# The last scan group inside the chunk loop, and the output projection behind it in another order

## The chip, the cores and the metric

The kernel runs on one core of a Trainium2 chip. Five engines matter: TensorE (PE, with its weight loads PEld), VectorE (DVE), ScalarE (ACT), GpSimd (POOL) and SyncE (SP), which issues most transfers. The metric is the device time of one execution in microseconds, taken as the median of several runs. Everything is float32; a product is made of three matmuls on split operands (high part and rest), which the tables call `fp32r`.

## The reference, cut to what matters

The model has two layers on 1024 tokens of width 1024. Layer 0 is a gated MLP; layer 1 is a Mamba-2 SSD mixer with 8 groups (G) of 4 heads and chunks of 128 tokens. The change is all in layer 1 and behind it:

```python
proj = h @ w_in                      # z (2048), x, B, C (4096), dt
xbc = silu(causal_conv(xbc))
# for each chunk: y = diagonal part + C @ state + x * d_skip, then state = state * decay + B' @ x
gated = (y * silu(z)).reshape(..., 8, 256)
gated = rmsnorm(gated, norm_w)       # over each group's 256 columns
h = h + gated @ w_out                # (1024 x 2048) @ (2048 x 1024)
return rmsnorm(h, final_norm_w)
```

The scan over the chunks is serial for each group. The output projection needs all groups, each scaled by its own norm.

## The kernel before, in words

**Projections and scan.** Groups 0, 1, 3, 5 have their projections made and stored earlier. For the groups in `plain` (2, 4, 6, 7) a generator, `projections()`, makes the x and B/C columns while the scan runs. It yields after every 6 matmuls of 128x512; the document calls that a *fill unit*. There are `total = 128` units, of which `AHEAD = 16` run before the loop. `scans()` loops over 7 groups x 8 chunks = 56 chunks. In each, `pe_b(n)` does the chunk's products (tiles `yy` and `sp`), one unit follows, then `pe_a(n+2)` transposes for a later chunk (`tp`), the state is updated (L1612), the output is formed (`out`), the decays of chunk n+1 are turned into weights (L1573, tile `wl`), and a second unit runs. `want` fixes this pace: (n + f) / 56 of the units left. The order on each engine is the order in which the code is written (`manual_schedule`).

**The last group.** Group 7 is not in the loop. Behind it `z_last` makes group 7's gate columns (tile `az`, 96 matmuls), `last_steps` scans its 8 chunks, and `interleave` mixes those with products 1 and 7 of the output projection.

**Output projection.** `Out` forms the 1024 x 2048 x 1024 product as seven products of half-size blocks (Strassen's scheme in Winograd's form), here in the order 1, 7, 2, 6, 4, 5, 3. A is the gated activations in quadrants A00 to A11 (first index: token half; tile `ya`), B the weights (tile `wb`). A product has four quarters (c), each of 4 x 2 x 3 = 24 matmuls into `bo`; product 3 is done by `last_mm`. `prep(n, c)` loads what is missing, scales A by the group's norm (L1816, tile `rb`) and splits both operands (L109 to L112). One quarter is prepared ahead. Sums of blocks are made by accumulating transfers from POOL's queue (`add` at L745, `b12_plus` at L708); plain loads are on SP's queue. The scale of a group goes a long way: squares, a sum over channels by matmul (`pr`), a store to `ss_d`, a load to `sv`, a root, a store to `rs_d`, and a load of `rb` spread over all partitions.

Of the kernel before, what the change touches and what calls it, by code (L numbers as in the profile page):

```python
# [29 lines left out]
def kernel(  # L30
# [627 lines left out]
    class Out:  # L658
# [10 lines left out]
        ORDER = (1, 7, 2, 6, 4, 5, 3)  # L669

        def __init__(self, src, w, scale, res, accs, keep, ran):
            self.src, self.w, self.scale, self.res, self.accs, self.keep = src, w, scale, res, accs, keep
            self.ran, self.had, self.late = ran, set(), []
# [11 lines left out]
        def load_a(self, i, kh, c):  # L685
# [5 lines left out]
            if self.scale is None:  # L691
                nc.sync.dma_start(out=raw, in_=src)
            else:
                self.scale(raw, src, g, i)
# [21 lines left out]
        def prep(self, n, c):  # L716
# [7 lines left out]
            x, y = A(i, j, c), B(k, l, c)  # L724
            xh, xl = (sb.tile([P, 2, 512], F32R, name=m, tag="wr", bufs=4) for m in ("xh", "xl"))
# [4 lines left out]
            if n == 1:  # L730
                self.add(x, self.src[c][:, :, 512:1024] if self.scale is None else A(1, 0, c))
                if self.scale is None:
                    if c % 2:
                        self.b12_plus(1, c // 2)
                elif c == 2:
                    self.b12_plus(1, 0)
            elif n == 7:
                if c == 0 and self.scale is not None:
                    self.b12_plus(1, 1)
# [7 lines left out]
        def sums(self, n, c):  # L747
# [7 lines left out]
            elif n == 4:  # L755
                if self.scale is not None:
                    if c % 2 == 0:
                        self.b12_plus(0, c // 2)
                    self.add(A(1, 0, c), A(1, 1, c))
                else:  # L760
                    if c == 1:
                        self.b12_plus(0, 1)
                    nc.vector.tensor_tensor(out=A(1, 0, c), in0=A(1, 0, c), in1=A(1, 1, c), op=ALU.add)

        def fetch(self, n, c):

            need = {1: (("a", 0, 0), ("b", 0, 0), ("b", 0, 1)), 11: (("a", 0, 0), ("b", 0, 0)),
                    2: (("a", 0, 1), ("b", 1, 0)), 22: (("a", 1, 1),), 4: (("b12", 0, 1),),
                    5: (("b", 1, 1),)}.get(n, ())
            if n in ((4,) if self.scale is None else (1, 11)):  # L770
                need += ("a", 1, 0),
            for kind, i, k in need:
                at = kind, i, k, c if kind == "a" else c // 2
                if at not in self.had:
                    self.had.add(at)
# [901 lines left out]
    def last_steps():  # L1677
# [8 lines left out]
        for c in range(8):  # L1686
            if c < 7:
                a(c + 1)
                yield
# [260 lines left out]
```

## Time and profile before

| | |
|---|---|
| median of 3 runs | 1596.49 us (1592.2 to 1597.92) |
| profiled execution | 1599.88 us |
| its span | 1598.2 us |
| TensorE / DVE / ACT / POOL busy | 1506.0 / 1055.3 / 777.0 / 418.7 us |
| chunk loop | from about 1069 to 1361 us |
| z projection of group 7 (`az`) | 1361 to 1392 us |
| output projection (`bo`) | 1392 to 1590 us |

Tables of stages give busy time and number of instructions for each engine. A group's row gives the line, engine, operation, output <- input, shape and count, then the total and mean duration, then the idle time ahead of it and what ended it. A busy TensorE is not one at its peak: matmuls overlap, so the spacing of their starts tells the pace.

### The profile page before, as it was taken

Reading aid. Unit: us, or ns where it says so; the run is one execution under the profiler, and the core shown is the slowest. Engines: PE = TensorE matmul, PEld = TensorE weight load, DVE = VectorE, ACT = ScalarE, POOL = GpSimd, SP = SyncE. Lnnn points to the kernel's source line nnn. Section 1 sums busy time; section 2 is a strip of 40 time slices with the busy share of each in tenths; the row PEclk is TensorE's granted clock in tenths of the full one; section 3 lists DMA queues with packets and bytes.
Section 4 is the critical chain, followed back from the end, with each engine's and each line's share of the span. In section 5 each row is a group of like instructions: output and inputs, shape, how many; then the busy total and the mean of one; then the engine's idle time right before and its main releaser. Section 6 shows DMA issues by size and latency. Waiting matters only on the chain.

```text
span 1598.2 us, 21253 instructions
## 1 busy us (share of the span) xinstructions
PE 1506.0 (94%) x7834; PEld 1239.8 (78%) x7834; DVE 1055.3 (66%) x1706; ACT 777.0 (49%) x1247; POOL 418.7 (26%) x443
## 2 busy tenths in 40 slices
PE   5799999999999999998999999989999999979988
PEld 4799988888888887876788787767777777757766
DVE  7966566666666554777637377757777767658656
ACT  4522233323222354555555455646766677544444
POOL 3601010000000131220011312126777765231231
PEclk7999999999999999999999999999999999989999
DMA  5153332332333999755367878776565665795992
GB/s 173 41 191 127 105 109 100 110 111 97 111 108 125 323 261 256 162 139 129 105 154 177 165 165 158 174 208 194 156 176 160 194 172 145 238 249 174 229 237 107
DMA packets 176919, 260.21 MB, mean 163 GB/s; under 512 B 16320, under 2 KB 102960, under 8 KB 173616
## 3 DMA queue, kind: packets, MB, share of 16 engines
q1 hardware_dynamic: 124992, 169.45, 34.3%
q0 software_dynamic: 41888, 71.58, 23.0%
q10 hardware_dynamic: 9936, 17.83, 3.1%
q8 instruction: 62, 1.02, 0.3%
q14 instruction: 41, 0.34, 0.1%
HBM read 185.61 MB, written 51.18 MB: 148 GB/s over the span
## 4 chain that ended last, share of the span: by engine, by line
PE 59%; issue 14%; DMA 9%; DVE 9%; ACT 6%; POOL 1%; ACTq 0%; SPq 0%; POOLq 0%; DVEq 0%
PE acc L136 10%; PE acc L134 9%; PE acc L135 9%; PE ab L134 4%; PE ab L136 4%; PE ab L135 4%; DMA ya<-ya 2%; PE yy L1582 2%; DMA wl<-cs_d 2%; PE yy L1586 2%; PE ao L134 2%; PE ao L135 2%; PE ao L136 2%; PE sp L1593 2%; ACT wh L111 2%
## 5 line engine op out<-in xcount | busy, mean ns | idle before, releaser
L134 PE MATMUL acc<-hh,wh 128*128 128x512 f32 x868 | 343.9, 396 | 15.4 <-ACT u L292 7.6
L136 PE MATMUL acc<-hh,wl 128*128 128x512 f32 x868 | 341.6, 394 | 1.7 <-DVE wl L112 1.6
L135 PE MATMUL acc<-hl,wh 128*128 128x512 f32 x868 | 340.8, 393 | 0.0
L134 PEld LDWEIGHTS acc<-hh,wh 128*128 128x128 f32 x868 | 164.8, 190 | 52.3 <-ACT u L292 9.3
L112 DVE TENSOR_TENSOR wl<-wr,wh 128x1024 fp32r<-128x1024 f32 (+1 forms) x99 | 118.1, 1194 | 128.2 <-ACT wh L111 128.1
L136 PEld LDWEIGHTS acc<-hh,wl 128*128 128x128 f32 x868 | 164.5, 190 | 40.2 <-DVE wl L112 5.6
L135 PEld LDWEIGHTS acc<-hl,wh 128*128 128x128 f32 x868 | 164.8, 190 | 33.4
L111 ACT CAST wh<-wr 128x1024 fp32r<-128x1024 f32 (+1 forms) x113 | 116.4, 1030 | 102.8 <-PE acc L135 57.9
L292 ACT COPY u<-acc 128x512 f32<-128x512 f32 x117 | 67.7, 583 | 197.4 <-PE acc L136 195.7
L136 PE MATMUL acc<-wh,hl 128*128 128x256 f32 x448 | 130.4, 291 | 13.2 <-DVE hl L395 13.2
L134 PE MATMUL acc<-wh,hh 128*128 128x256 f32 x448 | 131.2, 293 | 3.8 <-DVE vt L331 2.5
L135 PE MATMUL acc<-wl,hh 128*128 128x256 f32 x448 | 129.7, 290 | 1.3 <-DVE wl L405 1.3
L134 PE MATMUL ab<-hh,wh 128*128 128x512 f32 x256 | 116.5, 455 | 1.4 <-ACT zt L977 1.4
L1555 ACT ACTIVATE wl<-wl,tk 128x128 f32<-128x128 f32 x256 | 81.9, 391 | 64.1 <-DMA wl<-cs_d 63.8
L135 PE MATMUL ab<-hl,wh 128*128 128x512 f32 x256 | 101.7, 397 | 3.2 <-DVE hl L112 3.2
L136 PE MATMUL ab<-hh,wl 128*128 128x512 f32 x256 | 102.1, 399 | 0.0
L136 PEld LDWEIGHTS acc<-wh,hl 128*128 128x128 f32 x448 | 88.9, 198 | 14.3 <-DVE hl L395 14.3
L134 PEld LDWEIGHTS acc<-wh,hh 128*128 128x128 f32 x448 | 89.1, 199 | 4.8 <-issue 2.9
L134 PE MATMUL bo<-wh,xh 128*128 128x512 f32 x192 | 80.1, 417 | 12.7 <-ACT xh L111 7.4
L135 PEld LDWEIGHTS acc<-wl,hh 128*128 128x128 f32 x448 | 89.0, 199 | 1.7 <-DVE wl L405 1.5
L111 ACT CAST xh<-ya 128x1024 fp32r<-128x1024 f32 x40 | 42.0, 1050 | 90.1 <-PE ao L135 41.7
L112 DVE TENSOR_TENSOR xl<-ya,xh 128x1024 fp32r<-128x1024 f32 x40 | 49.0, 1224 | 55.8 <-ACT xh L111 55.7
(324 smaller groups left out, 3286.4 us busy)
## 6 DMA issues: line engine op xcount, KB each, us to landing
wr<-in_a_w_in_dram SPq DMA_DIRECT2D x48, 512.0 KB, 3.8
wl<-cs_d SPq DMA_DIRECT2D x64, 256.0 KB, 6.2
wr<-in_b_w_in_dram SPq DMA_DIRECT2D x30, 512.0 KB, 6.2
ya<-ya POOLq DMA_DIRECT2D x24, 512.0 KB, 15.5
wb<-in_a_w_out_dram SPq DMA_DIRECT2D x10, 1024.0 KB, 15.1
wb<-in_b_w_out_dram SPq DMA_DIRECT2D x10, 1024.0 KB, 13.7
wr<-in_b_w_in_dram SPq DMA_DIRECT2D x36, 256.0 KB, 6.7
v<-v_d SPq DMA_DIRECT2D x8, 1024.0 KB, 4.7
```

The lines of the kernel that those rows point to most:

```text
L111: nc.scalar.copy(out=hi, in_=src)
L112: return (eng or nc.vector).tensor_tensor(out=lo, in0=src, in1=hi.bitcast(F32), op=ALU.subtract)
L134: nc.tensor.matmul(out=o, lhsT=l[0], rhs=r[0], start=start, stop=False, **kw)
L135: nc.tensor.matmul(out=o, lhsT=l[0], rhs=r[1], start=False, stop=False, **kw)
L136: nc.tensor.matmul(out=o, lhsT=l[1], rhs=r[0], start=False, stop=stop, **kw)
L292: nc.scalar.copy(out=self.u[n][:, i], in_=a)
L1555: nc.scalar.activation(wl[:, j, :], wl[:, j, :], AF.Relu, scale=-1.0, bias=tokc(2, c, self.g)[:, j:j + 1])
L1582: nc.tensor.matmul(out=yy[f * 64:(f + 1) * 64, pt * P:(pt + 1) * P], lhsT=w[:, j * 64:(j + 1) * 64], rhs=wl[:, j, :], start=True, stop=True)
L1586: nc.tensor.matmul(out=yy[:, 256 + pt * P:384 + pt * P], lhsT=self.state[c - 1][:, pt * P:(pt + 1) * P], rhs=self.x(3, c), start=True, sto ...
L1593: nc.tensor.matmul(out=sp[:, 0:256], lhsT=w[:, 512:640], rhs=w[:, 256:512], start=True, stop=True)
```

## The change

Group 7's scan joins the loop, which now has 64 chunks. Its gate columns become the last item of `projections()` (16 units, tile `ab`, Silu into its own tile `z`), and products of the output projection follow in the same stream of units. `want` is now in two parts: up to chunk 50 the 112 units left of `total`, then 20 more over the last 14 chunks (the 16 of z and 4 of product 1). Group 7 writes its output over its own x; two wide gate products (`gate_half`) behind the loop replace eight small ones. Its adds and carries move from DVE to POOL like those of the other groups.

The output projection runs in the order 1, 2, 7, 6, 4, 5, 3. Its loads, sums and norm steps are written out in `hook_b`, quarter by quarter; the scaling of A is split from its load (`ready`) and done later. A00 + A10 is summed in product 2 instead of 1, and A10 + A11 by DVE instead of POOL's queue. All scales of norms are stored from SP's queue.

```diff
+            self.order, self.had, self.late, self.raw = order, set(), [], {}
...
-                self.scale(raw, src, g, i)
+                self.raw[i, kh, c] = self.scale(raw, src, g, i)
+
+        def ready(self, i, kh, c):
+            if (i, kh, c) in self.raw:
+                self.raw.pop((i, kh, c))()
...
             elif n == 4:
-                if self.scale is not None:
-                    if c % 2 == 0:
-                        self.b12_plus(0, c // 2)
-                    self.add(A(1, 0, c), A(1, 1, c))
...
+                if c == 1:
+                    self.b12_plus(0, 1)
+                nc.vector.tensor_tensor(out=A(1, 0, c), in0=A(1, 0, c), in1=A(1, 1, c), op=ALU.add)
...
-        seq = [(g, kind) for g in plain for kind in ("x", "bc")]
+        seq = [(g, kind) for g in plain for kind in ("x", "bc")] + [(G - 1, "z")]
...
+            if kind == "z":
+                queue.append([lambda: nc.scalar.activation(sts[g][kind][:, m, :], a.rearrange("p a b -> p (a b)"),
+                                                           AF.Silu)])
+                return 1
...
+        def gate_half(self, th):
+            y = self.z(4 * th, 4)
+            V.tensor_tensor(out=y, in0=y, in1=self.st["z"][:, :, th * 512:(th + 1) * 512], op=ALU.mult)
...
+    bo = Out(gd, b_w_out, gscale, lambda t, nb: h1_d[t][:, nb * 512:(nb + 1) * 512], accs_b, False,
+             (1, 2, 7, 6, 4, 5, 3))
...
+    def hook_b(n, c):
+        last, get = end["scan"], bo.get
+        at = n, c
+        if at == (1, 0):
+            for k in (2, 3):
+                get("a", 0, 0, k)
+            get("b", 0, 0, 2)
+            for k in (0, 1):
+                get("a", 0, 1, k)
+            get("b", 1, 0, 0)
+        elif at == (1, 1):
+            get("a", 0, 1, 2), get("b", 1, 0, 2)
+            last.sum_b(), last.sum_c(0), last.squares(1)
+        elif at == (1, 2):
+            last.sum_b(), last.sum_c(1)
+            end["half"] = [group_rstd(G - 1, 0, 512)]
+            for k in (0, 1):
+                get("a", 1, 0, k)
+            get("b", 0, 1, 0)
+        elif at == (1, 3):
+            end["half"][0][0]()
+            end["half"].append(group_rstd(G - 1, 512, 512))
+        elif n == 2:
+            if c < 2:
+                end["half"][c][1]()
+            if c == 0:
+                end["half"][1][0]()
+                for k in (2, 3):
+                    get("a", 1, 0, k)
+                get("b", 0, 1, 2)
+            elif c == 1:
+                get("a", 0, 1, 3)
+            elif c == 2:
+                get("a", 1, 1, 0), get("a", 1, 1, 1)
+            if c % 2 == 0:
+                bo.b12_plus(1, c // 2)
+            bo.ready(1, 0, c)
+            bo.add(bo.a(0, 0, c), bo.a(1, 0, c))
+        elif n == 7:
+            if c == 0:
+                get("a", 1, 1, 2), get("a", 1, 1, 3)
+            bo.ready(1, 1, c)
+            bo.sums(2, c)
+        elif n == 6:
+            bo.sums(6, c)
+            if c % 2 == 0:
+                get("b12", 0, 1, c)
+            if c == 0:
+                end["fnwb"] = q4([P, D], "fnwb")
+                nc.sync.dma_start(out=end["fnwb"], in_=final_norm_w.partition_broadcast(P))
+            elif c == 3:
+                bo.b12_plus(0, 0)
+        elif n == 4:
+            bo.sums(4, c)
+            bo.post(2, c)
+            if c % 2:
+                get("b", 1, 1, c - 1)
...
-        chunks = [(g, c) for g in range(G - 1) for c in range(8)]
-        N = len(chunks)
+        chunks = [(g, c) for g in range(G) for c in range(8)]
+        N, M = len(chunks), 50
...
+        def fill():
+            yield from pj
+            yield from bo.product(1, hook_b)
...
+        def want(at):
+            if at < M:
+                return AHEAD + (total - AHEAD) * at // M
+            return total + 20 * (at - M) // (N - M)
...
+            elif n == N - 6:
+                end["scan"] = scan[G - 1]
+                for k in range(2):
+                    bo.get("a", 0, 0, k)
+                bo.get("b", 0, 0, 0)
+            elif n == N - 4:
+                bo.prep(1, 0)
...
+        sc = scan[G - 1]
+        sc.gate_half(0), sc.gate_half(1), sc.squares(0)
+        for _ in fl:
             pass
```

TensorE near the end of the loop. Before, every chunk has a unit (six `ab` matmuls, of which one set of three is shown) on each side of the transposes `tp`:

```order
L1593 MATMUL sp<-cw 128x256
L134 MATMUL ab<-hh,wh 128x512
L135 MATMUL ab<-hl,wh 128x512
L136 MATMUL ab<-hh,wl 128x512
...
L1549 MATMUL tp<-ident,x 128x128 x2
L1549 MATMUL tp<-ident,bc 128x128
L1550 MATMUL tp<-bc 128x128
L134 MATMUL ab<-hh,wh 128x512
...
L1582 MATMUL yy<-wl,cw 64x128 x4
```

In the changed program, in chunk 60, the next chunk's `yy` stands right behind the transposes:

```order
L1579 MATMUL sp<-cw 128x256
L134 MATMUL ab<-hh,wh 128x512
L135 MATMUL ab<-hl,wh 128x512
L136 MATMUL ab<-hh,wl 128x512
...
L1535 MATMUL tp<-ident,x 128x128 x2
L1535 MATMUL tp<-ident,bc 128x128
L1536 MATMUL tp<-bc 128x128
L1568 MATMUL yy<-wl,cw 64x128 x4
```

The second unit is missing there; this holds for eight of the last 14 chunks (in some the first unit is the missing one).

DVE at the top of that chunk, in the changed program (L1549 and L1551 belong to a later chunk, L1598 is the state update, L1693 the scaling of A):

```order
L1549 TENSOR_TENSOR cw<-tp,tk 128x256
L1551 TENSOR_TENSOR cw<-tp,mask 128x128
L1693 SCALAR_TENSOR_TENSOR ya<-ya,par,rb 128x512 x2
L112 TENSOR_TENSOR xl<-ya,xh 128x1024
L112 TENSOR_TENSOR wl<-wb,wh 128x1024
L1598 TENSOR_TENSOR state<-sp,state 128x256
```

The scaling and splits of product 1's first quarter, which ran behind the loop, now stand ahead of a chunk's state update.

SP's queue in products 1 and 2 of the changed program, with the semaphores waited for (`srow` holds sums of group 7, `rvv` its roots, `g_d` the gated groups):

```order
L1650 DMA ss_d<-srow 2x256 [waits DMAHW4_49,Activation_49]
L1658 DMA sv<-ss_d 128x4 [waits DMAHW6_49,DMAHW4_49]
L1680 DMA rb<-rs_d 128x2x512 [waits PE_49]
L1688 DMA ya<-g_d_8250 128x2x512 [waits DMAHW0_49]
...
L1668 DMA rs_d<-rvv 128x4 [waits DMAHW3_49,DVE_49]
L1680 DMA rb<-rs_d 128x2x512 [waits PE_49,Pool_49]
L1688 DMA ya<-g_d_9110 128x2x512
```

The store of group 7's sums (waits for ACT) and of its roots (waits for DVE) are now ahead of the loads of A10 in the same queue; before, one root store was on POOL's queue and one on ACT's.

292 lines of the change are left out of this document (93 added, 199 removed).

## The prediction, made before the run

> **What bounds the kernel now.** I read the views in this order: busy time by stage, what TensorE waited for, its pace while it runs, then the transfers. The first fence is the view of stages (time from the span's start, then busy time and instructions of PE, PEld, DVE, ACT and POOL, granted clock, DMA share, GB/s). The cuts are mine: the chunk loop, group 7's z projection, products 1 and 7 beside the last scan, products 2, 6, 4 and most of 5, the end of 5 with product 3.
>
> ```profile
> core 0: us, PE busy (x) PEld busy (x) DVE busy (x) ACT busy (x) POOL busy (x), PEclk, DMA share, GB/s
> 1069.00:1361.00 292.00, 285.19 (x1739) 216.78 (x1738) 210.08 (x448) 196.21 (x420) 198.74 (x226) 0.99 0.60 167
> 1361.00:1392.00 31.00, 28.61 (x141) 22.53 (x140) 19.92 (x35) 15.98 (x22) 7.41 (x7) 0.94 0.73 245
> 1392.00:1467.20 75.20, 64.13 (x319) 48.36 (x318) 50.86 (x99) 32.81 (x53) 15.16 (x16) 0.91 0.79 204
> 1467.20:1556.00 88.80, 80.81 (x337) 64.94 (x335) 53.63 (x71) 43.59 (x55) 28.09 (x31) 0.96 1.06 241
> 1556.00:1590.20 34.20, 34.10 (x143) 27.85 (x143) 24.94 (x49) 17.32 (x33) 4.00 (x4) 0.95 0.30 98
> ```
>
> In the loop TensorE is busy 285 of 292 us, DVE 210: TensorE bounds it. From 1361 to 1590.2 (229.2 us) it is busy 207.65 us and stands 21.5 us, beside DMA engines whose share reaches 1.06. The view of waits from 1361 to 1600, TensorE alone, says for what (total us, times, longest):
>
> ```profile
> PE bo L134 <- ACT xh L111: 7.4, 2, 4.2
> PE bo L134 <- ACT wh L111: 5.2, 3, 2.2
> PE bo L135 <- DVE wl L112: 4.9, 4, 2.0
> PE pr L1645 <- POOL gsq L1638: 2.4, 1, 2.4
> PE pr L1645 <- ACT gsq L1633: 1.1, 1, 1.1
> PE bo L136 <- DVE xl L112: 0.5, 1, 0.5
> ```
>
> 18 of the 21.5 us are operands of the output projection that were not split in time. The standing costs more than itself. The timeline gives the pace at full clock (51 z matmuls, first and last, so 11.33 / 50 = 0.2266 us each) and a stop; the chain of waits gives the pace just behind that stop, 0.43 us.
>
> ```profile
> 1361.09 0.39 PE L134 MATMUL az<-hh,wh 128*128 128x512 f32 x1
> 1372.42 0.39 PE L136 MATMUL az<-hh,wl 128*128 128x512 f32 x1
> ...
> 1496.12 0.50 PE L134 MATMUL bo<-wh,xh 128*128 128x512 f32 x1 [1.92 <-ACT wh L111]
> ```
>
> ```profile
> 1498.14 0.43 PE bo L136
> 1498.57 0.43 PE bo L134
> ```
>
> **The change part by part.** Same work on TensorE: z is 96 matmuls, seven products 672; 768 x 0.2266 = 174.0 us. A scan chunk's own TensorE work comes from the loop: 112 fill units of 6 matmuls (1.36 us each) are 152.3 of its 285.19 busy us, and 132.9 / 56 chunks = 2.37 us. Eight chunks are 19.0. So 193.0 us at full clock stand against 207.65 busy: 14.6 us (estimate) went to the half-rate stretches behind stops. If every stop after 1361 went, 21.5 + 14.6 = 36.1 us would go and the span would be 1598.2 - 36.1 = **1562.1**. That is the base; the rest asks which stops the new order makes.
>
> *First 50 chunks: 0.* They take 112 units instead of 100, 2.24 x 1.36 + 2.37 = 5.42 us a chunk, TensorE-bound as before; DVE's 210.08 / 56 = 3.75 us hides under it, more so than at 2 units.
>
> *Last 14 chunks.* They have 20 units: by the order eight chunks have one and six have two. One chunk's dependent work stands in the timeline:
>
> ```profile
> 1254.09 0.69 DVE L1573 TENSOR_TENSOR wl<-wl,cw 128x512 f32<-128x512 f32 x1
> ...
> 1256.57 0.60 PE L1593 MATMUL sp<-cw 128*128 128x256 f32 x2
> 1257.27 0.42 DVE L1612 TENSOR_TENSOR state<-sp,state 128x256 f32<-128x256 f32 x1 [0.77 <-POOL cw L1568]
> 1258.40 0.38 PE L1549 MATMUL tp<-ident,x 128*128 128x128 f32 x2
> 1258.45 1.78 DVE L1573 TENSOR_TENSOR wl<-wl,cw 128x512 f32<-128x512 f32 x1
> 1258.87 0.48 PE L134 MATMUL ab<-hh,wh 128*128 128x512 f32 x1
> 1260.41 0.66 PE L1582 MATMUL yy<-wl,cw 128*64 128x128 f32 x8
> ```
>
> The end of sp (1257.17) to the start of the weights product L1573 is 1.28 us, and its end (1260.23) to the next yy 0.18. With L1573 at its mean (0.981, row below) the chain takes 2.44 us. One unit and the transposes (1258.40 to 1258.87, 0.47) cover 1.83: 0.61 short, eight times, **5 us**. Ends: 0, if its fast records (0.69 in the first row) and earlier slack serve, and 11 at the 1.78 of this row.
>
> Into the same chunks come two operand preparations of product 1. From the groups of the loop and, for the last four rows, of 1392 to 1568.6 (busy, mean ns | idle before):
>
> ```profile
> L1573 DVE TENSOR_TENSOR wl<-wl,cw 128x512 f32<-128x512 f32 x55 | 54.0, 981 | 8.2 <-ACT wl L1557 8.1
> L1612 DVE TENSOR_TENSOR state<-sp,state 128x256 f32<-128x256 f32 x42 | 17.8, 425 | 62.3 <-PE sp L1593 34.2 <-ACT srow L1649 15.6 <-PE ab L136 5.2
> ...
> L112 DVE TENSOR_TENSOR wl<-wb,wh 128x1024 fp32r<-128x1024 f32 x23 | 28.4, 1236 | 0.0
> L112 DVE TENSOR_TENSOR xl<-ya,xh 128x1024 fp32r<-128x1024 f32 x18 | 22.0, 1224 | 20.9 <-ACT xh L111 20.8
> L1816 DVE SCALAR_TENSOR_TENSOR ya<-ya,par,rb 128x512 f32<-128x512 f32 x20 | 14.4, 748 | 14.8 <-DMA rb<-rs_d 7.9 <-DMA ya<-g_d 6.9
> ...
> L111 ACT CAST xh<-ya 128x1024 fp32r<-128x1024 f32 x18 | 18.9, 1049 | 47.1 <-PE bo L135 21.1 <-DMA ya<-ya 12.6 <-issue 12.1
> ```
>
> Two scalings, two splits and the wait for xh are 1.50 + 1.22 + 1.24 + 1.05 = 5.0 us ahead of the next state update, on a DVE that idles 62.3 / 42 = 1.5 us a chunk there: up to 3.5 short each. I take 2.5 each, since the chunk before is a two-unit one: **5 us**, ends 0 and 7. The loads that feed them are issued two and more chunks (9 us) ahead.
>
> *Behind the loop.* Half 0's gate product (1024 elements, nearest row L112, 1.22), its square (ACT, nearest xh, 1.05), t1, x terms and the four small rstd steps (some 2.6 together, bounded by 1 and 3.5) come before the sum over half 0, that is 4.9 us, with two units, 2.7, above them: **2 us**, ends 1 and 4. The 2.4 and 1.1 us of the old sums are gone.
>
> *Product 2.* It now runs before 7 and carries, for each quarter, four scalings and two splits on DVE: 4 x 0.748 + 2.46 = 5.45 us against 24 x 0.2266 = 5.44 of matmuls. Nothing is left for the small rstd steps of group 7's halves or a late load: **4 us**, ends 0 and 10.
>
> *Transfers.* The rows of 1380 to 1600 (packets, MB, share; then sizes and time to landing):
>
> ```profile
> q0 software_dynamic: 7360, 19.93, 47.9%
> q1 hardware_dynamic: 13423, 25.05, 32.7%
> ...
> ya<-ya POOLq DMA_DIRECT2D x16, 512.0 KB, 14.3
> wb<-wb POOLq DMA_DIRECT2D x8, 512.0 KB, 11.5
> wb<-in_b_w_out_dram POOLq DMA_DIRECT2D x4, 1024.0 KB, 16.3
> u<-h_d POOLq DMA_DIRECT2D x12, 256.0 KB, 16.0
> ```
>
> POOL's accumulating transfers run at 19.93 MB / (0.479 x 220 us) = 189 GB/s, SP's loads at 348. Between the end of z and the last sum that product 4 reads, the new order moves 16.8 MB of loads (48 us) and, by its POOL rows, 13.4 MB of accumulation (71 us): 119 us, or 112 at the share of 1.06. TensorE needs from there 2.8 chunks (6.6), products 1, 2, 7, 6 (87) and three quarters of 4 (16.3), less 4 for preparing: 106 us, and 119 with my stops behind z. So I take **0**; 13 if the share is 1.0 and no other stop gives time. Four sums of 512 KB that POOL's queue did for product 5 (A10 + A11, 11 us of DMA) are with DVE now and not among them.
>
> On this the Trainium skill ("DMA: Bandwidth & Descriptors", section "Anatomy of one DMA — SWDGE (gpsimd) path") fits a POOL-issued DMA as 2.0 us plus bytes over 436 GB/s, 3.2 us for 512 KB; by it the 13.4 MB would need some 31 us and transfers could not matter. The rows (14.3 us, 189 GB/s) disagree with it for accumulating ones, so the sum keeps the rows.
>
> *Half clock.* Six stops cost 14.6 us before, 2.4 each. Of the new ones four are long enough (two preparations, the sum, product 2) at 1.7 to 2.4: **7 us**, ends 0 and 14. The Trainium skill ("TensorE: Matmul & The Clock Gate", section "What's actually happening") halves the clock only after about 3.4 us idle; by it my stops would cost nothing here and the sum would be 1578. The stop at 1496 (1.92 us, then 0.96) was followed by 0.43 us matmuls all the same, so the rows stay.
>
> Sum: 5 + 5 + 2 + 4 + 0 + 7 = 23; span 1562.1 + 23 = **1585**. The profiled run took 1599.88, 1.7 more than its span and 3.4 more than the median 1596.49; the timed median is thus the span less 1.7: **1583 us**, 0.8% faster.
>
> **The rivals.**
> *A, the tail of the loop hides its chains* (0.18). L1573's fast records and slack of two-unit chunks cover both terms: stops of 2 and 2 and one half-rate stretch of 2, span 1568, timed 1566. For: the loop lost under 7 us in 56 chunks. Against: in the rows above the weights end 0.18 us before their matmul even with two units.
> *B, the stops only move* (0.22). 11 + 7 + 3 + 6 + 9: 36 us, span 1598, timed 1596, no change. For: DVE would be the bound in the tail and in product 2 alike.
> *C, slower: SP's queue in product 2* (0.15). Group 7's sums and scales now sit on SP, in order, ahead of the loads for the next quadrant. The view of waits of SP's queue from 1360 to 1600:
>
> ```profile
> SPq L1652 <- ACT srow L1649: 29.4, 3, 12.9
> SPq L1805 <- DMA rs_d<-rvv: 12.6, 1, 12.6
> ```
>
> If such waits (12.9 + 12.6) come one after the other while product 2 needs those loads on DVE, TensorE stands some 25 us more: span 1610, timed 1608. It decides once the chain from sum to scaled operand is longer than the 22 us of a product. Against: the sums are taken early in product 1, and the scale is needed only in product 2's last quarter.
>
> **How the numbers follow.** My forecast has 0.43 (own range 1575 to 1592), A 0.18, B 0.22, C 0.15; 0.02 is for a scan that is bound otherwise from the start. About 0.5% (8 us) is what this measurement tells from no change, so faster means below 1588.5. Of my own range 0.38 lies there, with A 0.56; same is 0.05 + 0.22 = 0.27; slower C and the rest, 0.17. The range 1566 to 1602 leaves out half of C and a little below A, under 2 in 10.
>
> **What would show it.** Right: no az matmuls, loop chunks of 5.4 us up to chunk 50; then short TensorE waits for L1573's successor in one-unit chunks; two waits of 2 to 4 us at the preparations; product 2 with DVE busy throughout; products 7, 6, 4 without stops though the DMA share stays near 1. Wrong: TensorE waiting in products 6 or 4 for ya<-ya or wb<-wb (then transfers decide), SP's queue waiting over 10 us for srow or rvv in product 2 (C), or no wait at all between chunk 50 and product 1 (A).

## The result, and the profile after

The change makes the kernel slower: **1615.79 us** median of 4 runs (1613.06 to 1621.55) beside 1597.01 us for the kernel before on the same chip, ratio **1.0129, 95% interval 1.0094 to 1.0163**. Measured once more (the first run below) it gave 1.0089 (1.0069 to 1.0108). The forecast was 1583 us, 0.8% faster, and the range ended at 1602.

The profiled execution took 1621.55 us, its span is 1619.8. The view of stages of the kernel after (columns as in the prediction: time from the span's start, then busy time and instructions of PE, PEld, DVE, ACT and POOL, granted clock, DMA share, GB/s). The cuts are mine: the first 50 chunks; the last 14 chunks with product 1's first quarter; the rest of product 1; product 2; products 7 and 6; products 4 and 5.

```profile
core 0: us, PE busy (x) PEld busy (x) DVE busy (x) ACT busy (x) POOL busy (x), PEclk, DMA share, GB/s
1070.70:1358.20 287.50, 273.12 (x1627) 208.57 (x1626) 188.66 (x406) 182.59 (x378) 185.96 (x205) 0.98 0.55 155
1358.20:1433.60 75.40, 63.35 (x390) 47.52 (x389) 50.65 (x116) 44.89 (x92) 37.70 (x46) 0.93 0.61 195
1433.60:1451.30 17.70, 17.70 (x83) 13.83 (x82) 11.39 (x14) 10.40 (x14) 1.45 (x1) 1.00 0.68 230
1451.30:1484.70 33.40, 25.34 (x98) 19.71 (x97) 18.69 (x29) 15.86 (x17) 7.69 (x8) 0.85 0.82 208
1484.70:1531.20 46.50, 43.93 (x194) 35.76 (x192) 27.08 (x29) 18.91 (x20) 17.25 (x20) 1.00 1.07 218
1531.20:1590.20 59.00, 48.73 (x192) 37.94 (x193) 41.36 (x55) 27.90 (x43) 9.76 (x11) 0.94 0.84 187
```

The time is lost in four places. The first 50 chunks take 287.5 us where the pace before (261.1 us) and 12 more units of 1.36 us make 277.4: 10.1 us too many. Behind chunk 50 TensorE stands 12.1 us in the last chunks (75.40 - 63.35), 8.1 in product 2, 2.6 in 7 and 6, and 10.3 in 4 and 5: 33.0 us. From 1358.2 to 1590.2 it is busy 199.05 us; at full clock its work there is 14 x 2.37 + 20 x 1.36 + 23 quarters x 5.44 = 185.5, so 13.5 us went to the half clock. 10.1 + 33.0 + 13.5 = 56.6, and 1562.1 (the prediction's base) + 56.6 = 1618.7: the span, but for 1.1 us.

What TensorE waited for, from three answers of the view of waits (total us, times, longest): chunks 0 to 50, then 50 to the end of product 1's first quarter, then the output projection.

```profile
PE yy L1568 <- issue: 7.3, 4, 5.3
PE ab L134 <- DVE x L1278: 3.8, 2, 1.9
PE ab L134 <- DVE bc L1278: 1.9, 1, 1.9
PE yy L1568 <- ACT wl L1543: 1.3, 1, 1.3
...
PE yy L1568 <- issue: 6.4, 1, 6.4
PE yy L1568 <- DVE wl L1559: 3.2, 1, 3.2
PE yy L1568 <- ACT wl L1543: 1.6, 1, 1.6
...
PE bo L134 <- ACT wh L111: 10.7, 3, 7.1
PE bo L135 <- DVE wl L112: 5.1, 5, 2.6
PE bo L134 <- DVE u L858: 2.5, 1, 2.5
PE bo L134 <- ACT u L852: 1.8, 1, 1.8
...
```

The same view of the kernel before shows 5.8 us of waits in chunks 0 to 50:

```profile
PE yy L1582 <- ACT wl L1557: 3.7, 2, 2.0
PE yy L1582 <- PE ab L136: 1.8, 3, 0.6
...
```

After, two kinds are new: `ab` waiting for the convolution's taps (the PSUM pair of the last piece is not read yet), and long waits of `yy` whose cause the view only calls "issue". The timeline shows what is behind the 6.4 us one, chunk 60 (SP, DVE, ACT and PE rows, put in order of engine):

```profile
1392.57 1.24 SPq L1688 DMA_DIRECT2D ya<-g_d  x2
1393.91 1.21 SPq L706 DMA_DIRECT2D wb<-in_b_w_out_dram  x1
1395.22 1.32 SPq L1530 DMA_DIRECT2D wl<-cs_d  x2
...
1406.11 1.28 ACT L1541 ACTIVATE wl<-wl,tk 128x128 f32<-128x128 f32 x4 [5.23 <-DMA wl<-cs_d]
1408.24 1.05 ACT L111 CAST xh<-ya 128x1024 fp32r<-128x1024 f32 x1
...
1403.29 1.76 DVE L1693 SCALAR_TENSOR_TENSOR ya<-ya,par,rb 128x512 f32<-128x512 f32 x2
1409.32 1.23 DVE L112 TENSOR_TENSOR xl<-ya,xh 128x1024 fp32r<-128x1024 f32 x1 [4.27 <-ACT xh L111]
1412.78 0.68 DVE L1559 TENSOR_TENSOR wl<-wl,cw 128x512 f32<-128x512 f32 x1
...
1413.56 1.12 PE L1568 MATMUL yy<-wl,cw 128*64 128x128 f32 x8 [6.36 <-issue]
```

Product 1's early loads are issued ahead of the decay load `wl<-cs_d` (the second of the two at 1395.22), which lands 10 us after its issue. ACT stands on it for 5.23 us; the operand's high half `xh` is queued behind; DVE has scaled the operand and stands 4.27 us for `xh`, and behind DVE's low half are the state and the weights that the chunk itself needs. Each engine keeps the order in which the code is written, so a late decay load of a later chunk stops this one.

### The profile page after: what moved, and what is told of

Same layout as the page of the kernel before. It is cut to its first block, busy times and chain, and to the rows that moved or that the text cites. A ratio compares the mean times of both kernels' runs of the same rounds, so it can differ in the third digit from the quotient of the medians.

```text
span 1619.8 us, 21233 instructions
## 1 busy us (share of the span) xinstructions
PE 1511.3 (93%) x7834; PEld 1244.2 (77%) x7834; DVE 1047.6 (65%) x1689; ACT 782.7 (48%) x1250; POOL 428.2 (26%) x452
## 3 DMA queue, kind: packets, MB, share of 16 engines
q10 hardware_dynamic: 9792, 17.83, 3.0%
## 4 chain that ended last, share of the span: by engine, by line
PE 49%; issue 20%; DVE 11%; DMA 11%; ACT 7%; POOL 1%; ACTq 0%; SPq 0%; POOLq 0%; DVEq 0%
PE acc L136 8%; PE acc L134 8%; PE acc L135 8%; PE ab L134 4%; PE ab L136 4%; PE ab L135 4%; DMA wb<-in_b_w_out_dram 3%; PE yy L1568 2%; PE yy L1572 2%; DMA ya<-ya 2%; DVE wl L112 2%; PE ao L134 2%; PE ao L135 2%; PE ao L136 2%; ACT wh L111 2%
## 5 line engine op out<-in xcount | busy, mean ns | idle before, releaser
L135 PEld LDWEIGHTS acc<-hl,wh 128*128 128x128 f32 x868 | 164.8, 190 | 33.4
L134 PE MATMUL ab<-hh,wh 128*128 128x512 f32 x288 | 130.3, 452 | 8.9 <-DVE x L1278 3.8
L135 PE MATMUL ab<-hl,wh 128*128 128x512 f32 x288 | 114.2, 397 | 1.6 <-DVE hl L112 1.6
L136 PE MATMUL ab<-hh,wl 128*128 128x512 f32 x288 | 115.0, 399 | 0.0
L135 PE MATMUL bo<-wl,xh 128*128 128x512 f32 x192 | 78.2, 407 | 5.1 <-DVE wl L112 5.1
## 6 DMA issues: line engine op xcount, KB each, us to landing
ya<-ya POOLq DMA_DIRECT2D x20, 512.0 KB, 15.5
```

Of the source, the lines that this page charges most:

```text
L134: nc.tensor.matmul(out=o, lhsT=l[0], rhs=r[0], start=start, stop=False, **kw)
L135: nc.tensor.matmul(out=o, lhsT=l[0], rhs=r[1], start=False, stop=False, **kw)
L136: nc.tensor.matmul(out=o, lhsT=l[1], rhs=r[0], start=False, stop=stop, **kw)
```

## The experiments

The runs are named by their labels. Each ratio is to the kernel before on the same chip, with its 95% interval; the change itself is the yardstick, at 1.0089 to 1.0129. The stage times are of the profiled executions.

**The change again.** No edit.

> The change itself once more, as the yardstick for the small differences: ratio to before 1.010 to 1.014, chunk 0 to 50 in 283 to 288 us, product 1's second quarter to product 3 in 155 to 158 us.

Measured: 1.0089 (1.0069 to 1.0108), chunks 0 to 50 in 286.2 us, product 1's second quarter to product 3 in 156.9. The ratio is a little below what was expected, the stages repeat, and over both measurements the change is slower by 0.7 to 1.6%. Nine profiled executions with the same first 50 chunks took 282.9 to 289.7 us there, 285.1 in the mean.

### The first 50 chunks

**The rate alone**, in the kernel before:

```diff
-            want = lambda f: AHEAD + (total - AHEAD) * (n + f) // N
+            want = lambda f: AHEAD + (total - AHEAD) * min(n + f, 50) // 50
```

> The kernel before with one number changed: its 112 fill units are spread over the first 50 of its 56 chunks (2.24 a chunk), and the last 6 chunks have none. Theory (the denser fill alone costs, since ACT, DVE and the decay loads then fall behind at some chunks): chunk 0 to 50 takes 283 to 287 us, as in the change (mean 285 of nine runs with the same first 50 chunks), against 261.1 + 12 x 1.36 = 277.4; the last 6 chunks then take 15 to 20 us instead of 31. Rival (something else of the change, not the rate, slows the loop): 276 to 279 us, with the waits of the kernel before.

Measured: 283.3 us for chunks 0 to 50, ratio 1.0029 (1.0011 to 1.0046). Its waits of TensorE in them:

```profile
PE yy L1582 <- issue: 6.5, 4, 4.5
PE ab L134 <- DVE x L1281: 3.8, 2, 1.9
PE ab L134 <- DVE bc L1281: 1.9, 1, 1.9
PE yy L1582 <- ACT wl L1557: 0.4, 1, 0.4
```

These are the changed kernel's waits, one by one and in the same chunks, in a kernel in which nothing but the pace differs. 2.24 units a chunk instead of 2 cost 6 of the 7.7 us (285.1 - 277.4), and the rest is less than the spread of the nine.

**The queue of convolution steps.** `drain()` takes one step per chunk; a piece of 8 units now lasts 3.6 chunks and has four to five.

```diff
-            drain()
+            drain(2 if n < M else 1)
```

> Up to chunk 50 two convolution operations leave the queue per chunk instead of one; nothing else changes. Theory (the denser fill outruns the one-per-chunk queue, so a PSUM pair is not free when the next block begins): the three 1.9 us waits of TensorE for the convolution's taps (1256.6, 1299.0, 1340.5) go, chunk 0 to 50 takes 280 to 283 us instead of 287.5, the median falls by 4 to 8 us to 1608-1612. Rival (DVE and SP are simply fuller at 2.24 units a chunk): the waits move to other operations, 286 to 288 us stay, median 1614-1618. Under both the 5.3 us wait near 1227 stays, since it ends with a load on SP.

Measured: 1.0133 (1.0112 to 1.0154), 283.9 us. The three 1.9 us waits are gone, as expected, but waits of `yy` grew from 7.3 to 12.9 us in total. 283.9 us lies between theory and rival and inside the spread of the nine; the ratio shows no gain, as the rival said. At the longest new wait (4.65 us, chunk 41) DVE stands 4.29 us for the convolution's step on ACT and does the chunk's weights product only behind it: what left the queue earlier stood in front of the chunk's own work.

**The bursts of loads.** The gate and decay loads of each group two chunks behind those of x, B and C:

```diff
-            if c == 0:
-                prefetch(g, 1)
+            if c in (0, 2):
+                if g < G - 1:
+                    prefetch(g, 1, c // 2)
+                elif c == 0:
+                    prefetch(g, 1)
```

(Part 0 holds x, B and C, part 1 the gate and the decays. Chunks 4 and 6 do the same for the next group; group 7's loads stay as they were.)

> The change with one thing moved: of each scan group's loads (x/B/C, gate and decays: 1.5 to 2 MB in one go) the gate and the decays are issued two chunks later than x/B/C. Theory (in the first 50 chunks the small decay loads of the next chunks stand behind these bursts on SP, and the denser fill puts weight loads on top of them): the waits near chunk 28 and 36 (1.3 to 5.3 us, ending with a decay load) go, chunk 0 to 50 takes 276 to 281 us instead of 284 to 290, the median falls by 5 to 9 us. Rival (the burst's bytes, not their order, or DVE and SP fullness): 284 to 290 us stay, the waits move to other chunks, median within 3 us of the change.

Measured: 1.0045 (1.0023 to 1.0067), 280.1 us, within the theory. The first line is ACT ahead of the 5.3 us wait near chunk 28 of the kernel after, the second the waits of `yy` in this run:

```profile
1220.46 1.28 ACT L1541 ACTIVATE wl<-wl,tk 128x128 f32<-128x128 f32 x4 [6.32 <-DMA wl<-cs_d]
...
PE yy L1570 <- issue: 3.6, 3, 1.8
```

The wait near chunk 28 is 1.8 us, the one near chunk 44 is 0.2; the three 1.9 us waits for the taps stay. The four combinations below, with the same move, took 280.1 to 282.6 us. So some 3 to 5 of the loop's 8 us were decay loads landing late behind bursts.

**The weight splits on POOL.** The groups of DVE's work show one instruction with two durations: `L1559` takes 0.71 us in 39 of 50 cases and 1.81 in the 11 that overlap a 2.39 us weight split on POOL.

```diff
-                split(*W[i, kh], raw.pop((i, kh)), nc.gpsimd if i else V)
+                split(*W[i, kh], raw.pop((i, kh)), V)
```

> The change with the fill's weight splits (the low half of each 128x1024 piece, 2.39 us on POOL, 14 in the first 50 chunks) done on DVE, where the same form takes 1.22 us. Theory (DVE's instructions with operands in SBUF stand while such a split runs on POOL: the weights product takes 1.8 us beside one and 0.7 alone, a 128x8 step 2.3 instead of 0.2): DVE gives 17 us of its own time but loses these stretches, the 1.9 us waits behind them shrink, chunk 0 to 50 takes 279 to 283 us instead of 285; ratio 1.004 to 1.009. Rival (DVE has no room for another 1.22 us in the chunk where it falls, or the waits come from the loads): 285 to 290 us, waits of TensorE for DVE's wl; ratio 1.010 to 1.015.

Measured: 1.0097 (1.0064 to 1.0130), 285.1 us. Groups of DVE's work in the first 50 chunks, first of the kernel after, then of this run (busy us, mean ns):

```profile
L1559 DVE TENSOR_TENSOR wl<-wl,cw 128x512 f32<-128x512 f32 x50 | 47.6, 952 | 0.7 <-ACT wl L1543 0.6
```

```profile
L1559 DVE TENSOR_TENSOR wl<-wl,cw 128x512 f32<-128x512 f32 x50 | 35.2, 705 | 0.7 <-ACT wl L1543 0.7
L112 DVE TENSOR_TENSOR wl<-wr,wh 128x1024 fp32r<-128x1024 f32 x14 | 19.7, 1408 | 17.6 <-ACT wh L111 16.8
```

The blocking is real and goes (12.4 us of DVE in the weights product alone), but the splits cost 19.7 us there, and TensorE's waits are nearly the same (one of 5.0 us and the three of 1.9 are still there). The ratio is between the two that were expected, the time the rival's: what DVE won by this did not shorten the loop.

### Chunk 60 and product 1

**Product 1 out of the loop**, its early loads left where they were:

```diff
-            return total + 20 * (at - M) // (N - M)
+            return total + 16 * (at - M) // (N - M)
...
             elif n == N - 4:
-                bo.prep(1, 0)
+                pass
```

> No part of product 1 runs inside the loop: the preparation at chunk 60 is gone, the last 14 chunks get the 16 z units, and product 1 begins behind the loop. The early loads (two pieces of A, one of B) stay where they are. Theory (the preparations' DVE and ACT work, in order ahead of the chunk's chain, made the waits of 6.4 and 3.2 us): both waits go, but the two preparations now stand open behind the loop for about 5 us; the median falls by 4 to 7 us to 1609-1612. Rival (the 2.5 MB of early loads in front of the chunk's small decay load made them): a wait of 4 to 6 us stays near chunk 60, and the open preparations come on top; median 1617-1622.

Measured: 1.0111 (1.0083 to 1.0139). A 3.0 us wait stays near chunk 60 with no preparation there, and 6.9 us stand open in front of product 1. About half of the wait is the loads', and the work moved out only stands elsewhere: closer to the rival.

**The early loads one by one**, at chunks 55, 57 and 59 instead of all at 58 (the preparation stays at 60).

> The change with product 1's first loads (1 MB of B, two pieces of A) issued one by one at chunks 55, 57 and 59 instead of all at chunk 58. Theory (the 2 MB burst holds back the decay load of chunks 60 and 61 on SP: without product 1 in the loop half of that wait was still there): the 5.5 to 6.4 us wait at chunk 60 shrinks to under 3 us, the decay load lands in time; median 2 to 5 us below the change. Rival (the preparation's work on DVE and ACT alone makes it): the wait stays at 4 to 6 us, median as the change.

Measured: 1.0087 (1.0056 to 1.0117). Waits of 3.8 and 1.8 us instead of one of 6.4, the 3 us one at the second preparation as before, chunk 50 to product 1's second quarter 74.1 us: nothing gained that can be told from the yardstick.

**The preparation at the last chunk**, 16 units in the last 14 chunks:

```diff
-            elif n == N - 4:
+            elif n == N - 1:
                 bo.prep(1, 0)
```

> The change with product 1's first preparation at the last chunk (63) instead of chunk 60, and only the 16 z units in the last 14 chunks. Theory (in chunks 60 and 61 the preparation's scalings and splits stand in order ahead of work that the next chunk needs; in the last chunk nothing in the loop waits behind them, and the last z units cover them): the 5.5 to 6.4 us wait shrinks to the 3 us that the early loads alone make, the 3 us wait at chunk 63 goes, and product 1 begins with a wait of under 3 us; chunk 50 to product 1's second quarter takes 68 to 71 us instead of 74 to 75; median 4 to 6 us below the change. Rival (the work stands open behind the loop wherever it is put): 73 us and more, median within 2 us of the change.

Measured: 71.1 us for that stretch, near the theory (68 to 71; the change 75.3 and 76.3), but ratio 1.0099 (1.0075 to 1.0124). The next stages took it back: from product 1's second quarter to product 3 161.9 us instead of 156.6 (the runs that left these stages as they were took 154.6 to 157.9).

### Product 2 and the chain of scales

Group 7's row of scales is the last operand of product 2. After, in the timeline (SP, DVE and PE rows):

```profile
1456.58 0.34 SPq L1668 DMA_DIRECT2D rs_d<-rvv  x1
...
1463.49 0.33 SPq L1668 DMA_DIRECT2D rs_d<-rvv  x1
1463.91 0.92 SPq L1680 DMA_DIRECT2D rb<-rs_d  x2
...
1471.89 1.41 DVE L1693 SCALAR_TENSOR_TENSOR ya<-x,par,rb 128x512 f32<-128x512 f32 x2 [7.11 <-DMA rb<-rs_d]
...
1475.44 0.79 PE L134 MATMUL bo<-wh,xh 128*128 128x512 f32 x1 [7.08 <-ACT wh L111]
```

The first half's scales are stored at 1456.58, but their load leaves at 1463.91: in front of it in SP's order stands the store of the second half's, which waits for DVE. SP's own waits show it, 4.8 us here, and before it 11.3 us in front of the first store (its line names `sv`, which DVE writes right behind the roots `rvv`):

```profile
SPq L1668 <- DVE sv L1662: 11.3, 1, 11.3
SPq L1668 <- DVE rvv L153: 4.8, 1, 4.8
```

**Without the chain:** group 7 takes group 6's row.

```diff
-        rb = weights(g, th)
+        rb = weights(min(g, G - 2), th)
```

> Diagnostic that leaves out a dependence: group 7's gated outputs are scaled with group 6's row of scales, which is long there, so nobody waits for group 7's chain (sum, store, load, root, store, load); the output is not the reference's in this. Theory (the chain through SP's queue costs its whole wait): the 7.1 us wait in product 2 goes, product 2 takes 22 to 24 us instead of 33.4, the sums behind it start earlier too, and the median falls by 8 to 12 us to 1604-1608. Rival (the accumulating transfers decide when product 5 begins): product 2 is shorter but products 4 and 5 wait longer for their operands, and the median falls by 0 to 4 us to 1612-1616.

Measured: 1.0080 (1.0063 to 1.0098). Product 2 falls from 33.4 to 25.6 us, and product 7 rises from 22.6 to 29.0. Most of the wait is given back one product later: there ACT now waits up to 9.3 us for the POOL accumulations A00 + A10 (`ya<-ya`), which product 7 reads. That is the rival's mechanism, one place earlier than it said.

**The load one quarter earlier, ahead of that store:**

```diff
-            if c < 2:
-                end["half"][c][1]()
             if c == 0:
+                end["half"][0][1]()
...
+                get("a", 0, 1, 3)
             elif c == 1:
-                get("a", 0, 1, 3)
+                end["half"][1][1]()
```

> The change with the load of group 7's first row of scales issued in product 2's first quarter, ahead of the store of the second half's scales, instead of behind it. Theory (SP's in-order queue holds the load back by 6 us behind a store that waits for DVE): the 7.1 us wait in product 2 shrinks to 1 to 3 us and product 2 takes 27 to 29 us instead of 33; behind it products 7 to 5 give back about half, as in the run without the wait; median 2 to 5 us below the change. Rival (the load is late because of the chain before it, or lands late under the other loads): the wait stays over 5 us, median as the change.

Measured: 1.0064 (1.0042 to 1.0087); product 2 in 27.1 us, product 7 in 29.5. The order on SP did make the wait (1.3 us are left of 7.1). Product 7 takes back all of the 6 us won there, product 4 is 3 us shorter, and 3 us are left at product 3 (153.5 us from product 1's second quarter instead of 156.6). That is the theory, size included, though the 3 us are no more than the spread of the runs that changed nothing there (154.6 to 157.9).

### Products 4 and 5

The chain of waits of the kernel after, from product 7 on (start, us, engine, what):

```profile
1484.67 11.40 DMA ya<-ya
1496.17 0.90 ACT xh L111
1497.08 13.21 DMA wb<-wb
1510.34 17.91 DMA wb<-in_b_w_out_dram
1528.27 1.92 ACT wb L711
1530.48 28.19 DMA wb<-in_b_w_out_dram
1558.69 1.05 ACT wh L111
```

SP's own waits in the same stretch name what the reload stood for:

```profile
SPq L706 <- DMA wb<-wb: 50.2, 2, 37.2
```

B12's reload needs a free tile. It gets one when product 7's accumulation B11 + (B22 - B12) has landed (1497.08 + 13.21 = 1510.3). Then come reload, negation and accumulation, one after the other, and product 5 starts at 1559.8.

**Without that accumulation:**

```diff
-                if c == 1:
-                    self.b12_plus(0, 1)
+                pass
...
-            elif c == 3:
-                bo.b12_plus(0, 0)
```

> Diagnostic that leaves out work: the two 1 MB accumulations that make product 5's right operand (B12 reloaded minus B11) are not done, so the output is not the reference's; the reload stays. Theory (these two transfers, 28 and some 10 us from issue to use, decide product 5's first quarters): the waits at 1559.8, 1569 and 1579 (7 to 8 us with their half clock) shrink to under 2 us, products 4 and 5 take 45 to 48 us instead of 59; the median falls by 8 to 12 us to 1604-1608. Rival (the accumulations of A and of the other B pieces in front of them decide as well, or ACT and DVE): the stops move to products 6 and 4, and the median falls by 0 to 4 us to 1612-1616.

Measured: 1.0047 (1.0031 to 1.0063), with the spread loads the largest gain of a single edit; products 4 and 5 in 53.8 us instead of 59.0, and the 1.8 us wait in front of product 4 is gone. That is between theory and rival: the two products took 15.5 us more than their 43.5 of matmuls, and 5.2 of them are these accumulations'. A wait of 1.7 us for a right operand stays (the chain of waits now runs over the accumulations `ya<-ya`, 15.94 us, and `wb<-wb`, 23.34), and so does the one of 2.5 for `u`, the sums that are read from the accumulators.

**The scan part alone:** group 7 in the loop, the old order of products behind it, without product 1 in the loop.

```diff
-    bo = Out(..., (1, 2, 7, 6, 4, 5, 3))
+    bo = Out(..., (1, 7, 2))
...
+            yield from bo.product(7, hook_b)
...
-        for n in (2, 7, 6, 4, 5):
+        for n in (2, 6, 4, 5):
```

(The order itself is 1, 7, 2, 6, 4, 5, 3; the tuple names the products that run up to the loop's end. `hook_b` fetches and sums as the kernel before did, but issues the loads of products 1 and 2 a quarter to a product ahead of their scaling.)

> The scan part of the change alone: group 7 in the chunk loop, fill by count, z among the projections; behind the loop the output projection goes in the order before (1, 7, 2, 6, 4, 5, 3) with its old sums on POOL, only its loads are issued early enough; no part of product 1 in the loop. Theory (the order 1, 2, 7 costs twice: product 2's last quarter comes too early for group 7's scale, and product 7's pieces of B come free only two products ahead of product 5, while reload, negation and accumulation need over 60 us): from product 1's second quarter to product 3 it takes 130 to 142 us instead of 156.6, no wait over 3 us in products 2 to 5; the loop and product 1 stay as slow as in the change; ratio to before 0.995 to 1.005, that is 15 to 25 us faster than the change. Rival (the transfers of this stage are too many in any order once the scan no longer runs beside them): 150 us and more, waits of TensorE in products 2, 6 or 4 for loads or accumulations, ratio 1.008 to 1.018.

Measured: 1.0037 (1.0018 to 1.0055); from product 1's second quarter to product 3 145.8 us instead of 156.6. That lies between theory and rival. Products 2 and 6 have no wait left, product 7 one of 2.0 us; waits of 2.8 and 3.1 us stay in product 5, and products 4 and 5 take 55.5 us, only 3.5 less than in the change. Ahead of them POOL waits 16.2 us for ACT's negation of B12, and the chain of waits has 20.1 us of the accumulation A10 + A11 (which is on POOL's queue again here; the expectations below call it A21 + A22).

### Putting the pieces together

**The changed order with four moves:** two queue steps per chunk, the spread loads, the earlier row of scales, the preparation at the last chunk.

> The change with four moves together: two queue operations per chunk up to chunk 50, the groups' gate and decay loads two chunks later, group 7's first row of scales loaded ahead of the store of the second half, and product 1's first preparation at the last chunk. Theory (the losses are separate and add up, half of each being given back downstream): chunk 0 to 50 in 275 to 279 us, to product 1's second quarter 69 to 72, from there to product 3 151 to 154; ratio 0.998 to 1.004. Rival (what is won early is given back in products 4 and 5, where the reload chain of B12 decides): products 4 and 5 take over 60 us; ratio 1.004 to 1.010.

Measured: 1.0064 (1.0041 to 1.0086); 282.6 and 71.4 us up to product 1's second quarter, then 159.3 to product 3, and products 4 and 5 together 59.3. The ratio is the rival's: what is won early is given back. But it is given back in product 7 (30.7 us instead of 22.6), not in products 4 and 5 as the rival said.

**The old order with its own moves:** on top of the scan part alone the spread loads, two queue steps, the late preparation, later sums over group 7's halves, earlier negations, A10 + A11 on DVE.

> The scan in the loop with the old order of the output projection, and these moves: two queue operations per chunk, gate and decay loads two chunks later, product 1's first preparation at the last chunk, the sums over group 7's halves a quarter later, the negations of the reloaded B12 a quarter earlier, A21 + A22 on DVE instead of POOL's queue. Theory (with the order's cost gone and each wait's cause moved, the loop's shorter scan tail remains as a gain): chunk 0 to 50 in 275 to 279 us, to product 1's second quarter 70 to 74, from there to product 3 134 to 140; ratio 0.985 to 0.992, faster than before. Rival (transfers and DVE fullness bound products 2 to 5 in either order): 145 us and more behind product 1's first quarter; ratio 0.997 to 1.003.

Measured: 1.0018 (1.0002 to 1.0034), 148.3 us from product 1's second quarter to product 3. The numbers are the rival's, its mechanism is not: products 4 and 5 take 44.6 us, near their 43.5 of matmuls, but product 1 has a 6.7 us wait for weights, whose loads were issued behind a store that waits for DVE, and product 2 one of 3.4.

**And its last moves:**

```diff
             if n == N - 1:
+                for k in (2, 3):
+                    bo.get("a", 0, 0, k)
+                bo.get("b", 0, 0, 2)
+                for k in (2, 3):
+                    bo.get("a", 1, 0, k)
+                bo.get("b", 0, 1, 2)
                 bo.prep(1, 0)
```

with the half sums a quarter earlier again and one queue step per chunk. (What the expectation calls the wait in product 7 is the one in product 2.)

> The scan in the loop with the old order behind it, as in the combination before this one, with the loads of product 1's second half issued at the last chunk instead of behind it, the sums over group 7's halves taken a quarter earlier again, and one queue operation per chunk. Theory (the 6.7 us wait in product 1 was loads issued 9 us before their use behind a store that waits for DVE; the 3.4 us wait in product 7 was rows of scales queued behind late sums): both waits fall under 2 us, from product 1's second quarter to product 3 138 to 142 us instead of 148.3; ratio 0.993 to 0.998. Rival (DVE and SP are full there and the waits move on): 145 us and more, ratio 0.999 to 1.004.

Measured: **1585.1 us, ratio 0.9910 (0.9895 to 0.9925)**, faster than both kernels, and better than the theory: 134.0 us from product 1's second quarter to product 3. Three of its stages: the first 50 chunks; products 2, 6 and 4; product 5.

```profile
1067.80:1347.90 280.10, 270.55 (x1628) 206.55 (x1627) 188.21 (x406) 183.29 (x382) 185.83 (x206) 0.99 0.57 163
...
1465.00:1530.30 65.30, 65.30 (x289) 53.94 (x288) 49.39 (x58) 35.42 (x41) 22.89 (x25) 1.00 1.07 266
1530.30:1553.30 23.00, 22.68 (x97) 17.80 (x97) 19.50 (x27) 14.69 (x24) 0.86 (x1) 1.00 0.66 132
```

In products 2, 6 and 4 TensorE is busy 65.30 of 65.30 us while the DMA engines' share is 1.07. SP reloads B12 from 1468.08 on, 62 us ahead of product 5 (1530.35), where the change had 49.5:

```profile
1468.08 18.42 SPq L708 DMA_DIRECT2D wb<-in_b_w_out_dram  x2
```

**The same with the splits on DVE.**

> The best combination so far (scan in the loop, old order, early loads) with the same move of the fill's weight splits from POOL to DVE. Theory: chunk 0 to 50 in 274 to 278 us instead of 280, ratio 0.986 to 0.990. Rival: 280 to 285 us, ratio 0.990 to 0.996.

Measured: 0.9924 (0.9897 to 0.9950), 281.5 us for chunks 0 to 50: no gain here either.

## Why the prediction was wrong

By its own steps (predicted, then what the profile after shows):

| step | predicted, us | measured, us |
|---|---|---|
| first 50 chunks | 0 | 10.1 |
| chains in one-unit chunks | 5 | none; 1.6 at a decay load |
| two preparations | 5 | 9.6 (6.4 + 3.2) |
| sum behind the loop | 2 | 0.4 |
| product 2 | 4 | 8.1 |
| transfers (all waits in products 7, 6, 4 and 5) | 0 | 12.9 (2.6 + 10.3) |
| half clock | 7 | 13.5 |
| sum | 23 | 56.6, with 0.4 not named |

**The base and the kind of loss held.** Without the z stage the work at full clock is what the prediction counted, and three kinds of stop (preparations, product 2, half clock) are where it put them, each about twice the size. The base says what is there to win: the last combination, with the same work, has a span of 1582.9.

**"First 50 chunks: 0" failed.** It compared DVE's mean (3.75 us) with a chunk of 5.42. No engine is full on the average; what stopped TensorE are single chunks where a burst of loads holds back a decay load, or a piece's convolution falls on other work. The rate alone brought all these waits into the kernel before, and spreading the loads took 3 to 5 us of the 8 away.

**"Last 14 chunks: 5" failed to the good side.** The term used the weights product's mean of 0.981 us. That mean mixes 0.7 us alone with 1.8 beside a POOL split, and no split falls into these chunks: it ran at 0.74. A mean over two kinds of case had been taken for a duration.

**The preparations** were sized by work (5.0 us of scaling and splitting) with loads "two and more chunks ahead". The loads were in time for the preparation; they were in the way of a 256 KB decay load that the prediction did not count. The waits were 9.6 us instead of 5, and the run with the preparation left out still had 3 us of it.

**Product 2** went as rival C said, by SP's order, not by DVE's fullness: DVE is busy 18.69 of 33.40 us, and the sign that the prediction named for C, SP waiting over 10 us for group 7's roots, is there (11.3 us). C had 25 us by adding two waits of the kernel before; the place was right and the price 8, of which 1.3 remained once one load was moved ahead of one store. Little of this loss could be won back on its own: in the two runs without the wait product 7 took 29.0 and 29.5 us instead of 22.6.

**"Transfers: 0" failed, by the largest amount of the table.** It weighed bytes over rate: 119 us of transfer against 119 of TensorE, stops included, and it counted only up to the last sum that product 4 reads. Of the 10.3 us in products 4 and 5, 8.7 stand in product 5, behind that. The last combination moves the same 17.83 MB on POOL's queue behind chunk 50, has a DMA share of 1.07 in products 2, 6 and 4, and TensorE does not wait there at all; in the change it waits in products 4 and 5, where the share is 0.84. So it was not the sum of the bytes. The chain ahead of product 5 is one serial path: accumulation, a free tile, reload, negation, accumulation, 63 us from 1497 to 1560. With 7 third in the order, two products (43.5 us) lie between it and product 5; with 7 second, three do. How much of the 15.5 us that products 4 and 5 take beyond their matmuls is this path's is shown in part only: without its accumulations products 4 and 5 are 5.2 us shorter, in the old order alone 3.5 (there with A10 + A11 back on POOL's queue), in the old order with earlier negations and A10 + A11 on DVE 14.4. So the order had to change together with what stands in it. That the tile and not something else delays the reload is read from SP's wait; a tile more was not tried. The `u` waits (0.7 and 2.5 us for DVE, 1.8 for an ACT that stands behind the negation) are in this row too, and only the last of them can be traced to a transfer.

**Half clock.** 13.5 us lie at the end of the range given. The Trainium skill ("TensorE: Matmul & The Clock Gate", section "What's actually happening") ties the drop to some 3.4 us of idleness. Here the stage of products 4 and 5 has a granted clock of 0.94 and no stop above 2.8 us, so the rows still speak against that as a threshold.

**The rivals.** A's hidden chains are true for the one-unit chunks and for nothing else. B came to 36 us by other sizes of the same stops and, like the forecast, had nothing in the first 50 chunks nor in products 4 and 5, which are 20 of the 56.6 us by themselves. C's time of 1608 us was the nearest, though its mechanism carries 8 us of the difference.

## What to carry to other kernels

Where products are put in another order, follow each buffer, not only each sum: from its last reader, through reload and accumulation, to its next use, and compare that path's length with the matmuls between. A DMA share near 1 said nothing by itself here: the same bytes were hidden at a share of 1.07 in one order and left waits at 0.84 in another. And a small load that every chunk needs came late behind bursts issued ahead of it in the same queue (10 us at chunk 60), so here it paid to spread the bursts.

## What the hardware showed that was not expected

DVE stood while POOL ran a long instruction on SBUF. A 128x8 step that takes 0.17 us in the run with the splits on DVE took 2.29 here, until POOL's split was done (rows of DVE, then POOL, of the kernel after):

```profile
1299.28 2.29 DVE L152 TENSOR_SCALAR ru<-ru 128x8 f32<-128x8 f32 x1
...
1299.15 2.38 POOL L112 TENSOR_TENSOR wl<-wr,wh 128x1024 fp32r<-128x1024 f32 x1 [0.19 <-ACT wh L111]
```

The Trainium skill ("SBUF — State Buffer", section "Who interferes with whom") says that DVE and GpSimd share a port pair that one of them holds for a whole instruction; the trace agrees (the weights product 0.71 us alone, 1.81 in 11 overlapping cases), and the run with the splits on DVE removes it. What the blocking alone cost the kernel is not shown: moving the splits gave DVE more work than it freed, and no time was won.

An accumulating POOL transfer of 1 MB took 28.19 us to land in the change and, in the faster combination's chain of waits, 19.20, with the same 17.83 MB on POOL's queue in the whole stage.
